# A 2-layer encoder on one core: the mixer's output projection as seven block products in place of eight

## The chip, the cores and the metric

One core of a Trainium2 chip runs one program that computes both layers. The metric is the device time of one execution in microseconds. The kernel before was run three times for its time, and once more with the hardware profiler; the profiled execution has a time of its own.

## The reference, cut to what matters

Each layer does, on x (512 tokens x 1024 channels, float32):

```python
x = x + 0.5 * swiglu(rms_norm(x, ffn1_norm[l]), ffn1_w_in[l], ffn1_w_out[l])
x = x + token_mixer(rms_norm(x, mix_norm[l]), ...)      # ends with the lines below
x = x + 0.5 * swiglu(rms_norm(x, ffn2_norm[l]), ffn2_w_in[l], ffn2_w_out[l])
# token_mixer:
merged = gates[:, :, 0] * y_pool + gates[:, :, 1] * y_attn + gates[:, :, 2] * y_lru
return merged @ w_out                                    # 512x1024 by 1024x1024
```

After two layers there is one more RMS norm. The change is in `merged @ w_out`, once in each layer, and in how its result is added to x.

## The kernel before, in words

Every matrix product keeps float32 accuracy by a split: a float32 operand becomes a high part (ScalarE copies it to the rounded type fp32r) and a low part (VectorE subtracts the high part from the operand), and three matmuls (high by high, high by low, low by high) stand for one. Weights come from HBM into a buffer called `raw` (128x1024, 512 KB) and are split into `wh` and `wl`; the low part of merged and of other activations is made in the same way.

The work is a list of `Unit`s, each with a weight block, its matmuls (`mm`) and what follows them (`after`). The loop at the end of the program issues a unit's matmuls and then calls `gap`, which issues, in this order: what was put off with `later`, the unit's `after` (evictions of its result), the tasks that `defer(n, ...)` set for this gap, the ScalarE half of the split of the unit three ahead (`splits_to(done[-1] + 3)`), the side work of attention and the recurrence, what was put off with `later`, and the VectorE half of that split. Each engine runs its instructions in the order in which they are issued. After a split `loads()` fetches further blocks on SP's queue as far as the limit `held` lets it. All 128x1024 buffers come from one pool of 43 (`BIGS`); all matmul results from 8 PSUM banks.

The feed-forward networks already compute their products by a Strassen-Winograd scheme, in `seven`: the left operand A and the weight W are cut in 2x2 blocks, and seven block products P1, P2, Q5, Q3, P6, P7, Q4 take the place of eight. The left operands are A11, A12, A22 and the sums S1 = A21 - A22, S2 = S1 - A11, S3 = A11 - A21, S4 = A12 + S2. The sums of weight blocks are made by an accumulating DMA of the POOL queue (`add_fn`), which adds a block from HBM onto a `raw` that a product before has just been split from (`acc`): W11 becomes W11+W12 for Q5, then +W22 for P6, then +W21 for Q4, and W22 becomes W22+W12 for P7. The results are added to x block by block (`put`, `total`).

The output projection before is a plain product: for each column half (`ch` 1, then 0) four weight blocks of two 128-row slices, each a unit of 24 matmuls (4 row tiles x 2 slices x 3). In the second half the last two blocks' matmuls are held back, so that the row tiles 2 and 3 end first. `evict` then does x = 0.5 * result + x, one VectorE operation for each of the 8 row tiles, and calls `done(hh, ch)`, which starts the next feed-forward network on that quarter of x: squares for the norm on ScalarE, transposes on TensorE one gap later (`z_block`), and the sums and splits of z (`z_ready`). Merged's blocks are made by `y1(cpair)`, four units just ahead of the projection: gate times branch plus the other branches, then high and low part into `st["mg"]`.

In the profile, tiles are named by the program: `o` is the projection's result, `mg` merged, `y` a branch product, `zt`, `zf`, `zs`, `zh`, `zl` the next network's input (transposed, copied, summed, high, low), `P` and `Q` the block products. All instructions of the helpers have line 83, so the groups are told apart by tile names.

Of the kernel before, what the change touches and what calls it, by code (L numbers as in the profile page):

```python
# [17 lines left out]
S = 512  # L18
# [88 lines left out]
def trunk_kernel(ctx, tc, xn, pm, fin, cst, bd, f1i, f1o, win, wbp, wba, wbl, wout, f2i, f2o, out):  # L107
# [70 lines left out]
    x = {}  # L178
# [230 lines left out]
    LEFT = {"P1": "A11", "P2": "A12", "Q5": "S1", "Q3": "S4", "P6": "S2", "P7": "S3", "Q4": "A22"}  # L409

    def seven(order, nk, width, left, wap, after, held, prep=None, fresh=False):
# [6 lines left out]
        for p in order:  # L418
            name = LEFT[p]
            for n, (k0, k1) in enumerate(parts):  # L420
# [12 lines left out]
                elif p == "Q4":  # L433
                    block = b1[n]
                elif p == "P2":
                    block = Block([ld(1, 0)])
                elif p == "Q3":
                    block = b2[n] = Block([ld(1, 1)])
                    acc = ap(0, 1)
                else:  # L440
                    block = b2[n]
# [19 lines left out]
                units.append(Unit(block, flat((k1 - k0) * width), mm, fin, acc=acc, held=held[p] if isinstance(held, dict) else held, nk=k1 - k0))  # L461


    def ffn(wi, wo, done, order0, rf, lim0=12):
# [131 lines left out]
        comb, U, u, q5 = {}, {}, {}, {}  # L596
# [40 lines left out]
        def prep(p, n, i):  # L637
            if n % 2 == 0:
                sums, parts = combos(LEFT[p], n // 2)
                if LEFT[p] in ("S1", "S4", "S3"):  # L640
                    add_hook(i - 4, sums)
                add_hook(i - 3, parts)
            else:
                add_hook(i, lambda k=(LEFT[p], n // 2): comb.pop(k))

        def put(hh, kk, src, sign=1.0):
            for tt in range(2):
                xv = x[2 * (hh ^ rf) + tt, kk]
                V.scalar_tensor_tensor(out=xv, in0=src[tt], scalar=0.25 * sign, in1=xv, op0=MUL, op1=ADD)

        def copies(dst):
            def fn(ps):
                dst.update(enumerate(two("u")))
                for tt in range(2):
                    A.activation(out=dst[tt], in_=ps[tt], func=AF.Copy)
            return fn

        def total(ps):
            for tt in range(2):
                V.tensor_tensor(out=u[tt], in0=ps[tt], in1=u[tt], op=ADD)  # L660

        def o_p1(ps):
            copies(u)(ps)
            later.append(lambda: put(0, 0, u))

        def o_p2(ps):
            later.append(lambda: put(0, 0, ps))
            defer(1, lambda: done(0 ^ rf, 0))

        def o_q5(ps):  # L670
            copies(q5)(ps)
            later.append(lambda: put(0, 1, q5))
            defer(1, lambda: later.append(lambda: put(1, 1, q5)))
            defer(2, q5.clear)

        def o_q3(ps):
            later.append(lambda: put(0, 1, ps))

        def o_p6(ps):
            later.append(lambda: (total(ps), put(0, 1, u, -1.0)))  # L680
            defer(1, lambda: done(0 ^ rf, 1))

        def o_p7(ps):
            later.append(lambda: (total(ps), put(1, 1, u, -1.0)))
            defer(1, lambda: (later.append(lambda: (put(1, 0, u), u.clear())), done(1 ^ rf, 1)))

        def o_q4(ps):
            put(1, 0, ps)
            done(1 ^ rf, 0)
# [5 lines left out]
        def left(name, k):  # L695
# [3 lines left out]
              {"P1": o_p1, "P2": o_p2, "Q5": o_q5, "Q3": o_q3, "P6": o_p6, "P7": o_p7, "Q4": o_q4},  # L699
# [3 lines left out]
    def mixer(l, side, done, between):  # L703
# [344 lines left out]
        def after_gate(b, c):  # L1048
            def fn(ps):
                if c % 2 == 0:  # L1050
                    g["gt", b] = two("gt")
# [45 lines left out]
        def y1(cpair):  # L1097
# [18 lines left out]
            def after():  # L1116
                if cpair == 0:
                    st["mg"] = [None] * KD
                for s in range(2):
# [458 lines left out]
```

## Time and profile before

| what | before |
|---|---|
| time, median of three runs (lowest to highest) | 2153.4 us (2152.71 to 2156.05) |
| time of the profiled execution, its span | 2148.72 us, 2147.0 us |
| ScalarE and POOL busy | 1192.8 us, 343.4 us |
| bytes moved by DMA, mean rate | 314.61 MB, 147 GB/s |
| granted TensorE clock, mean | 0.995 |

The span runs from the first to the last instruction. "Busy" is the time in which at least one instruction of the engine runs; a matmul's record is longer than its share of the engine, since matmuls overlap, so that the pace is read from start to start. In a row of a timeline the bracket tells how long the engine stood idle before the instruction, and what ended the idle time. In the tables by stretch "x217" counts instructions.

### The profile page before, as it was taken

What the parts mean: (1) busy time and instruction counts of PE and PEld (TensorE: products, weight loads), DVE (VectorE), ACT (ScalarE), POOL (GpSimd) and SP (SyncE); (2) the same over time, 40 slices, a digit from 0 to 9 for tenths busy, and PEclk for the clock granted to TensorE, in tenths of its full rate; (3) what the DMA queues carried; (4) which work ended last, traced back from release to release, by engine and by line L of the source; (5) the groups of instructions that cost most, each with busy time, mean ns of one, the idle gap of its engine ahead of it and who ended that gap; (6) DMA issues with size and microseconds to landing.
All of it is one profiled execution on the core that took longest, in us unless ns stands there. A gap on an engine that the chain in (4) does not pass through costs nothing. (4 is left out here: it accounts for less than half of the span.)

```text
span 2147.0 us, 26106 instructions
## 1 busy us (share of the span) xinstructions
PE 2086.4 (97%) x9648; PEld 1735.6 (81%) x9648; DVE 1658.0 (77%) x2355; ACT 1192.8 (56%) x1763; POOL 343.4 (16%) x292
## 2 busy tenths in 40 slices
PE   7999999999999999999999999999999999999998
PEld 5888888788787878987878988877887877888786
DVE  5877898598677487779977778976967766877797
ACT  6554565646563554546665555565455536555564
POOL 1222230000000022322312222300000000222230
PEclk9999999999999999999999999999999999999999
DMA  8888896122225278898967889941221353888894
GB/s 224 181 153 191 196 200 180 50 79 88 67 81 172 78 141 169 165 200 206 207 162 142 170 179 232 185 127 60 79 79 59 116 154 84 175 151 193 203 177 106
DMA packets 194096, 314.61 MB, mean 147 GB/s; under 512 B 10544, under 2 KB 86832, under 8 KB 193968
## 3 DMA queue, kind: packets, MB, share of 16 engines
q0 software_dynamic: 76288, 138.43, 38.9%
q1 hardware_dynamic: 117680, 174.51, 24.9%
q8 instruction: 75, 1.23, 0.2%
q14 instruction: 53, 0.43, 0.1%
HBM read 310.80 MB, written 2.10 MB: 146 GB/s over the span
## 5 line engine op out<-in xcount | busy, mean ns | idle before, releaser
L83 DVE TENSOR_TENSOR wl<-raw,wh 128x1024 fp32r<-128x1024 f32 (+2 forms) x696 | 709.1, 1038 | 204.6 <-ACT wh L83 202.4
L83 ACT ACTIVATE wh<-raw 128x1024 fp32r<-128x1024 f32 (+2 forms) x696 | 610.5, 906 | 264.5 <-DMA raw<-in_f1i_dram 115.4
L83 PE MATMUL ps<-z,wh 128*128 128x512 f32 x1216 | 380.1, 393 | 0.0
L371 POOL DMA_DIRECT2D raw<-in_f2i_dram x96 | 115.9, 1223 | 1133.5 <-DVE wl L83 390.1
L83 PE MATMUL P<-wl,zh 128*128 128x512 f32 (+1 forms) x768 | 287.5, 374 | 8.3 <-DVE wl L83 8.3
L83 PE MATMUL P<-wh,zh 128*128 128x512 f32 (+1 forms) x768 | 286.9, 374 | 2.1 <-ACT wh L83 2.1
L83 PE MATMUL P<-wh,zl 128*128 128x512 f32 (+1 forms) x768 | 285.9, 372 | 0.0
L83 PEld LDWEIGHTS ps<-z,wh 128*128 128x128 f32 x1216 | 227.1, 188 | 51.0 <-issue 3.4
L83 PE MATMUL ps<-z,wl 128*128 128x512 f32 x608 | 237.0, 390 | 0.0
L83 PE MATMUL Q<-wl,zh 128*128 128x512 f32 (+1 forms) x576 | 218.5, 379 | 14.5 <-DVE wl L83 14.5
L83 PE MATMUL Q<-wh,zh 128*128 128x512 f32 (+1 forms) x576 | 221.0, 384 | 7.5 <-ACT zh L83 3.9
L83 PE MATMUL Q<-wh,zl 128*128 128x512 f32 (+1 forms) x576 | 217.1, 377 | 5.4 <-DVE zl L83 5.4
L371 POOL DMA_DIRECT2D raw<-in_f1i_dram x96 | 116.0, 1232 | 377.8 <-DVE wl L83 276.5
L83 PEld LDWEIGHTS P<-wl,zh 128*128 128x128 f32 x768 | 144.5, 188 | 33.7 <-DVE wl L83 14.0
L83 PEld LDWEIGHTS P<-wh,zh 128*128 128x128 f32 x768 | 144.5, 188 | 24.3 <-ACT wh L83 4.4
L83 PEld LDWEIGHTS P<-wh,zl 128*128 128x128 f32 x768 | 144.6, 188 | 19.6
L83 PE MATMUL P<-wl,ah 128*128 128x512 f32 x352 | 138.2, 393 | 3.3 <-DVE wl L83 3.1
L83 PEld LDWEIGHTS Q<-wl,zh 128*128 128x128 f32 x576 | 109.6, 190 | 37.1 <-DVE wl L83 22.9
L83 PE MATMUL P<-wh,ah 128*128 128x512 f32 x352 | 137.4, 390 | 0.0
L83 PE MATMUL P<-wh,al 128*128 128x512 f32 x352 | 137.2, 390 | 0.0
L83 PEld LDWEIGHTS ps<-z,wl 128*128 128x128 f32 x608 | 114.1, 188 | 23.7
L83 PEld LDWEIGHTS Q<-wh,zh 128*128 128x128 f32 x576 | 109.8, 191 | 25.1 <-ACT zh L83 5.6
(189 smaller groups left out, 3412.2 us busy)
## 6 DMA issues: line engine op xcount, KB each, us to landing
raw<-in_win_dram SPq DMA_DIRECT2D x84, 512.0 KB, 4.3
raw<-in_f1i_dram POOLq DMA_DIRECT2D x64, 512.0 KB, 7.2
raw<-in_f2i_dram POOLq DMA_DIRECT2D x64, 512.0 KB, 6.9
raw<-in_f2i_dram SPq DMA_DIRECT2D x52, 512.0 KB, 5.1
raw<-in_f1i_dram SPq DMA_DIRECT2D x50, 512.0 KB, 5.8
raw<-in_f1o_dram POOLq DMA_DIRECT2D x40, 512.0 KB, 8.0
raw<-in_f2o_dram POOLq DMA_DIRECT2D x40, 512.0 KB, 8.2
raw<-in_f1o_dram SPq DMA_DIRECT2D x30, 512.0 KB, 7.3
```

Of the source, the lines that this page charges most:

```text
L83: return fn(*args, **kw)
L371: return lambda raw: GP.dma_start(out=raw[:, 0:n * w].rearrange("p (k f) -> p k f", f=w), in_=src, accum_op=ADD)
```

## The change

The projection goes through `seven`, with merged as the left operand and `w_out` as the weight, both cut in 2x2 blocks (256 tokens x 512 channels; 512 x 512). A product is two units of 12 matmuls (2 row tiles x 2 slices x 3), in the order P1, P2, Q5, P7, P6, Q3, Q4. S1 to S4 of merged's blocks are made by `m_sum` from the float32 merged, which the gates' tiles keep in `st["mf"]`, in the gaps 1, 2, 4 and 6 behind the last `y1` (S1, S3, S2, S4), each with its own high and low part. Since P7 stands ahead of Q3, its block is loaded as W22 with W12 added at once, and Q3 loads W22 anew. The functions that add the products to x are moved out of `ffn` into `added`, shared by both; with `seventh` they take other orders. The row halves are exchanged (`rf = 1`): quarters of x are ready in the order A22 (behind P2), A11 (one gap behind P6), A21 (Q3), A12 (Q4).

```diff
-    LEFT = {"P1": "A11", "P2": "A12", "Q5": "S1", "Q3": "S4", "P6": "S2", "P7": "S3", "Q4": "A22"}
+    SEVEN = {"P1": "A11", "P2": "A12", "Q5": "S1", "Q3": "S4", "P6": "S2", "P7": "S3", "Q4": "A22"}
 
     def seven(order, nk, width, left, wap, after, held, prep=None, fresh=False):
...
                     block = b2[n] = Block([ld(1, 1)])
-                    acc = ap(0, 1)
+                    acc = ap(0, 1) if order.index("P7") > order.index("Q3") else None
+                elif order.index("P7") < order.index("Q3"):
+                    block = Block([ld(1, 1)], ap(0, 1))
                 else:
                     block = b2[n]

...
+    def added(scale, rf, done, seventh=False):
+
+
+        u, q5 = {}, {}
+
+        def put(hh, kk, src, sign=1.0):
+            for tt in range(2):
+                xv = x[2 * (hh ^ rf) + tt, kk]
+                V.scalar_tensor_tensor(out=xv, in0=src[tt], scalar=scale * sign, in1=xv, op0=MUL, op1=ADD)
+
+        def copies(dst):
+            def fn(ps):
+                dst.update(enumerate(two("u")))
+                for tt in range(2):
+                    A.activation(out=dst[tt], in_=ps[tt], func=AF.Copy)
+            return fn
+
+        def total(ps):
+            for tt in range(2):
+                V.tensor_tensor(out=u[tt], in0=ps[tt], in1=u[tt], op=ADD)
+
+        def p1(ps):
+            copies(u)(ps)
+            later.append(lambda: put(0, 0, u))
+            if seventh:
+                defer(1, lambda: later.append(lambda: put(0, 1, u, -1.0)))
+
+        def p2(ps):
+            later.append(lambda: put(0, 0, ps))
+            defer(1, lambda: done(0 ^ rf, 0))
+
+        def q5_(ps):
+            copies(q5)(ps)
+            later.append(lambda: put(0, 1, q5))
+            defer(1, lambda: later.append(lambda: put(1, 1, q5)))
+            defer(2, q5.clear)
+
+        def q3(ps):
+            if seventh:
+                put(0, 1, ps)
+                return done(0 ^ rf, 1)
+            later.append(lambda: put(0, 1, ps))
+
+        def p6(ps):
+            if seventh:
+                later.append(lambda: (total(ps), put(1, 1, u, -1.0), put(0, 1, ps, -1.0)))
+                return close22()
+            later.append(lambda: (total(ps), put(0, 1, u, -1.0)))
+            defer(1, lambda: done(0 ^ rf, 1))
+
+        def p7(ps):
+            if seventh:
+                return later.append(lambda: total(ps))
+            later.append(lambda: (total(ps), put(1, 1, u, -1.0)))
+            close22()
+
+        def close22():
+            defer(1, lambda: (later.append(lambda: (put(1, 0, u), u.clear())), done(1 ^ rf, 1)))
+
+        def q4(ps):
+            put(1, 0, ps)
+            done(1 ^ rf, 0)
+
+        return {"P1": p1, "P2": p2, "Q5": q5_, "Q3": q3, "P6": p6, "P7": p7, "Q4": q4}
...
                 if c % 2 == 0:
-                    g["gt", b] = two("gt")
+                    gt = big(name="gt")
+                    g["gt", b] = [gt[:, 0:S], gt[:, S:2 * S]]
+                    if b == 1:
+                        st["mf"][c // 2] = gt
...
+                if cpair == 3:
+                    defer(1, lambda: m_sum("S1"))
+                    defer(2, lambda: m_sum("S3"))
+                    defer(4, lambda: m_sum("S2"))
+                    defer(6, lambda: m_sum("S4"))
...
-        for ch in (1, 0):
-            box = {"held": []}
-            for u4 in range(4):
-                b = Block([load_fn(wout[l][u4 * 256:u4 * 256 + 256, ch * S:(ch + 1) * S].rearrange("(k p) f -> p k f", p=128), 2, S)])
-
-                def part(ts, box):
-                    for t in ts:
-                        for k0, uh, ul in box["held"]:
-                            for k in (k0, k0 + 1):
-                                wh, wl = (a[:, (k - k0) * S:(k - k0 + 1) * S] for a in (uh, ul))
-                                th, tl = (a[:, t * 128:(t + 1) * 128] for a in st["mg"][k])
-                                PE.matmul(box["ps"][t], lhsT=th, rhs=wh, start=k == 0, stop=False)
-                                PE.matmul(box["ps"][t], lhsT=th, rhs=wl, start=False, stop=False)
-                                PE.matmul(box["ps"][t], lhsT=tl, rhs=wh, start=False, stop=k == KD - 1)
-
-                def mm(u, a0, a1, u4=u4, ch=ch, box=box):
-                    if u4 == 0:
-                        box["ps"] = [bank("o") for _ in range(4)]
-                    box["held"].append((2 * u4, u.hi, u.lo))
-                    if ch == 0 and u4 >= 2:
-                        if u4 == 3:
-                            part((2, 3), box)
-                        return
-                    part(range(4), box)
-                    box["held"].clear()
-
-                def evict(hh, ch, box):
-                    for tt in range(2):
-                        t = 2 * hh + tt
-                        V.scalar_tensor_tensor(out=x[t, ch], in0=box["ps"][t], scalar=0.5, in1=x[t, ch], op0=MUL, op1=ADD)
-                    done(hh, ch)
-
-                def after(u4=u4, ch=ch, box=box):
-                    if u4 == 3:
-                        evict(1, ch, box)
-                        if ch == 1:
-                            evict(0, ch, box)
-                            box.clear()
-
-                units.append(Unit(b, flat(), mm, after, held=8))
-
-        def last_mm(u, a0, a1, box=box):
-            part((0, 1), box)
-            box["held"].clear()
-            st["mg"] = None
-
-        def last_after(box=box):
-            evict(0, 0, box)
-            box.clear()
-
-        units.append(Unit(None, [], last_mm, last_after))
+        rf = 1
+        sums = {}
+
+        def m_block(name):
+
+            if name in sums:
+                return [sums[name][:, j * S:(j + 1) * S].rearrange("p (c q) -> p c q", c=2) for j in range(2)]
+            r, k = (int(name[1]) - 1) ^ rf, int(name[2]) - 1
+            return [t.rearrange("p (c q) -> p c q", c=2)[:, :, r * 256:r * 256 + 256] for j in range(2) for t in (st["mf"][2 * k + j],)]
+
+        def m_sum(name):
+            a, b, op = {"S1": ("A21", "A22", SUB), "S2": ("S1", "A11", SUB), "S3": ("A11", "A21", SUB), "S4": ("A12", "S2", ADD)}[name]
+            a, b = m_block(a), m_block(b)
+            t = sums[name] = big(name="ms")
+            for o, p, q in zip(m_block(name), a, b):
+                V.tensor_tensor(out=o, in0=p, in1=q, op=op)
+            hi, lo = big(F32R, "mh"), big(F32R, "ml")
+            A.activation(out=hi, in_=t, func=AF.Copy)
+            later.append(lambda: V.tensor_tensor(out=lo, in0=t, in1=f(hi), op=SUB))
+            mc[name] = (hi, lo)
+            if name == "S4":
+                sums.clear()
+                st["mf"].clear()
+
+        mc = {}
+
+        def left(name, k):
+            if name[0] == "S":
+                return [a[:, k * 256:k * 256 + 256] for a in mc[name]]
+            r, c = (int(name[1]) - 1) ^ rf, 4 * (int(name[2]) - 1) + k
+            return [a[:, r * 256:r * 256 + 256] for a in st["mg"][c]]
+
+        def wap(r, c, k0, k1):
+            return wout[l][r * 512 + k0 * 128:r * 512 + k1 * 128, c * S:(c + 1) * S].rearrange("(k p) f -> p k f", p=128)
+
+        results = added(0.5, rf, done, True)
+
+        def then(p):
+            def fn(ps):
+                results[p](ps)
+                mc.pop(SEVEN[p], None)
+                if p == "P1":
+                    st["mg"][0:4] = [None] * 4
+                if p == "Q4":
+                    st["mg"] = None
+            return fn
+
+        seven(["P1", "P2", "Q5", "P7", "P6", "Q3", "Q4"], 4, S, left, wap, {p: then(p) for p in results}, 10)
```

In `ffn` the functions `o_p1` to `o_q4`, `put`, `copies` and `total` go, and `added(0.25, rf, done)` takes their place with the same operations.

## Rows read from the trace of the kernel before

**Rows 1.** Page, busy time by engine: busy us, share of the span, instructions.
```profile
PE 2086.4 (97%) x9648; PEld 1735.6 (81%) x9648; DVE 1658.0 (77%) x2355; ACT 1192.8 (56%) x1763; POOL 343.4 (16%) x292
```

**Rows 2.** Busy time by stretch: us, then each engine's busy us, PEclk, DMA share, GB/s.
```profile
692.20:738.30 46.10, 46.10 (x217) 38.48 (x216) 22.96 (x33) 19.37 (x36) 0.00 (x0) 1.00 0.34 99
738.30:781.00 42.70, 36.57 (x157) 27.49 (x155) 33.30 (x41) 25.11 (x36) 7.22 (x6) 1.00 0.65 144
1749.50:1795.60 46.10, 46.10 (x214) 38.35 (x213) 23.13 (x33) 19.08 (x35) 0.00 (x0) 1.00 0.35 100
1795.60:1838.00 42.40, 37.34 (x162) 28.18 (x160) 33.51 (x41) 26.13 (x38) 7.23 (x6) 1.00 0.66 148
```

**Rows 3.** Timeline of TensorE, layer 0: start, us, operation, count.
```profile
692.23 0.39 PE L83 MATMUL o<-wh,mg 128*128 128x512 f32 x1
...
719.43 1.91 PE L83 MATMUL zt<-cst,x 128*128 128x128 f32 x16
...
721.09 0.48 PE L83 MATMUL o<-wh,mg 128*128 128x512 f32 x1
...
738.31 0.47 PE L83 MATMUL P<-wh,zh 128*128 128x512 f32 x1
```

**Rows 4.** Timeline of VectorE, projection of layer 0: [idle before, releaser].
```profile
699.30 4.63 DVE L83 TENSOR_TENSOR wl<-raw,wh 128x1024 fp32r<-128x1024 f32 x4 [0.26 <-ACT wh L83]
...
712.82 0.69 DVE L83 SCALAR_TENSOR_TENSOR x<-o,x 128x512 f32<-128x512 f32 x1 [8.89 <-PE o L83]
...
733.75 0.16 DVE L83 TENSOR_TENSOR m<-m 128x2 f32<-128x2 f32 x1 [0.79 <-ACT q L83]
...
735.34 1.23 DVE L83 TENSOR_TENSOR wl<-raw,wh 128x1024 fp32r<-128x1024 f32 x1
```

**Rows 5.** Timeline of VectorE, first feed-forward block of layer 0.
```profile
743.38 1.22 DVE L83 TENSOR_TENSOR zs<-zf 128x1024 f32<-128x1024 f32 x1
...
745.72 1.22 DVE L83 TENSOR_TENSOR zl<-zs,zh 128x1024 fp32r<-128x1024 f32 x1 [1.12 <-ACT zh L83]
...
764.78 1.28 DVE L83 TENSOR_TENSOR c<-P,u 128x512 f32<-128x512 f32 x2
```

**Rows 6.** Groups by line and form: busy us, mean ns; idle before.
```profile
L83 ACT ACTIVATE wh<-raw 128x1024 fp32r<-128x1024 f32 x404 | 416.6, 1052 | 173.8 <-DMA raw<-in_f1i_dram 72.7 <-DMA raw<-in_f2i_dram 58.6 <-DVE wl L83 26.8
...
L83 ACT ACTIVATE u<-P 128x512 f32<-128x512 f32 x40 | 23.6, 604 | 29.5 <-PE P L83 29.2
```

**Rows 7.** Timeline of ScalarE, layer 0.
```profile
698.22 3.89 ACT L83 ACTIVATE wh<-raw 128x1024 fp32r<-128x1024 f32 x4
...
773.20 1.06 ACT L83 ACTIVATE wh<-raw 128x1024 fp32r<-128x1024 f32 x1 [3.12 <-DMA raw<-in_f2i_dram]
```

**Rows 8.** Timeline of TensorE, first feed-forward block of layer 0.
```profile
745.74 0.50 PE L83 MATMUL Q<-wh,zh 128*128 128x512 f32 x1 [0.81 <-ACT zh L83]
...
747.00 0.50 PE L83 MATMUL Q<-wh,zl 128*128 128x512 f32 x1 [0.52 <-DVE zl L83]
...
757.44 0.50 PE L83 MATMUL P<-wl,zh 128*128 128x512 f32 x1 [0.95 <-DVE wl L83]
```

**Rows 9.** DMA queues and issues (count, KB each, median us from issue to landing).
```profile
q0 software_dynamic: 76288, 138.43, 38.9%
q1 hardware_dynamic: 117680, 174.51, 24.9%
...
raw<-in_f2i_dram POOLq DMA_DIRECT2D x64, 512.0 KB, 6.9
...
raw<-in_f2o_dram POOLq DMA_DIRECT2D x40, 512.0 KB, 8.2
...
raw<-in_f2o_dram POOLq DMA_DIRECT2D x8, 256.0 KB, 10.4
```

More of the change, by code (lines that the diff above doesn't have):

```diff
@@ L418, in seven @@
         for p in order:
-            name = LEFT[p]
+            name = SEVEN[p]
             for n, (k0, k1) in enumerate(parts):
@@ L593, in ffn @@
         add_hook(nz, zc.clear)
-        comb, U, u, q5 = {}, {}, {}, {}
+        comb, U = {}, {}
         cols = [1024, 1024, 768]
@@ L638, in prep @@
             if n % 2 == 0:
-                sums, parts = combos(LEFT[p], n // 2)
-                if LEFT[p] in ("S1", "S4", "S3"):
+                sums, parts = combos(SEVEN[p], n // 2)
+                if SEVEN[p] in ("S1", "S4", "S3"):
                     add_hook(i - 4, sums)
@@ L643, in prep @@
             else:
-                add_hook(i, lambda k=(LEFT[p], n // 2): comb.pop(k))
-        def put(hh, kk, src, sign=1.0):
-            for tt in range(2):
[L648 to L689, printed above, removed]
+                add_hook(i, lambda k=(SEVEN[p], n // 2): comb.pop(k))
+        results = added(0.25, rf, done)
         def wap(r, c, k0, k1):
@@ L698, in ffn @@
         seven(later_order, KF // 2, S, left, wap,
-              {"P1": o_p1, "P2": o_p2, "Q5": o_q5, "Q3": o_q3, "P6": o_p6, "P7": o_p7, "Q4": o_q4},
+              results,
               dict(P1=12, P2=14, Q5=14, Q3=14, P6=14, P7=12, Q4=9), prep)
@@ L1180, in mixer @@
         units[n0].between = between
-        for ch in (1, 0):
-            box = {"held": []}
-            for u4 in range(4):
-                b = Block([load_fn(wout[l][u4 * 256:u4 * 256 + 256, ch * S:(ch + 1) * S].rearrange("(k p) f -> p k f", p=128), 2, S)])
-                def part(ts, box):
-                    for t in ts:
-                        for k0, uh, ul in box["held"]:
-                            for k in (k0, k0 + 1):
-                                wh, wl = (a[:, (k - k0) * S:(k - k0 + 1) * S] for a in (uh, ul))
-                                th, tl = (a[:, t * 128:(t + 1) * 128] for a in st["mg"][k])
-                                PE.matmul(box["ps"][t], lhsT=th, rhs=wh, start=k == 0, stop=False)
-                                PE.matmul(box["ps"][t], lhsT=th, rhs=wl, start=False, stop=False)
-                                PE.matmul(box["ps"][t], lhsT=tl, rhs=wh, start=False, stop=k == KD - 1)
-                def mm(u, a0, a1, u4=u4, ch=ch, box=box):
-                    if u4 == 0:
-                        box["ps"] = [bank("o") for _ in range(4)]
-                    box["held"].append((2 * u4, u.hi, u.lo))
-                    if ch == 0 and u4 >= 2:
-                        if u4 == 3:
-                            part((2, 3), box)
-                        return
-                    part(range(4), box)
-                    box["held"].clear()
-                def evict(hh, ch, box):
-                    for tt in range(2):
-                        t = 2 * hh + tt
-                        V.scalar_tensor_tensor(out=x[t, ch], in0=box["ps"][t], scalar=0.5, in1=x[t, ch], op0=MUL, op1=ADD)
-                    done(hh, ch)
-                def after(u4=u4, ch=ch, box=box):
-                    if u4 == 3:
-                        evict(1, ch, box)
-                        if ch == 1:
-                            evict(0, ch, box)
-                            box.clear()
-                units.append(Unit(b, flat(), mm, after, held=8))
@@ L1386, in between @@
             flush()
+        st["mf"] = {}
         mixer(l, side, to_ffn(g2, 0), between)
```

## The prediction

> **What bounds the kernel now.** I read the page's engine summary first: TensorE is busy for 97% of the span and VectorE for 77% [rows 1], which says that removed matmuls should pay, but it is a mean over stages. So I went to the busy time by stretch [rows 2], with the stretch edges taken from the first output-projection matmul of each layer and the first matmul of the feed-forward network behind it (692.2 and 738.3 us in layer 0; 1749.5 and 1795.6 in layer 1). In the projection TensorE is busy 46.1 of 46.1 us while VectorE is busy 23 of 46, so there TensorE alone sets the pace. In the first 43 us behind it TensorE has 6.1 us of gaps and VectorE is at 33.3 of 42.7: that seam is set by VectorE and the handovers between it and ScalarE. Third, the timelines of the engines. TensorE goes straight from 692.23 to 738.31 at 0.227 us a matmul (120 from 692.23 to the transposes at 719.43) [rows 3]. VectorE comes late into the stage: the last branch tiles' evictions hold it until 699.3, 7 us after TensorE began on the projection; then it does four weight splits in a row (4.63 us) and finds nothing more to do until 712.8 [rows 4]. So before the change the projection starts with VectorE about three units of work behind, and survives that because units here are 24 matmuls long (5.44 us) and a unit's split is made three units ahead.
>
> **The change, part by part.** All numbers are for one layer, for one profiled execution (2148.7 us around a span of 2147.0); it ran 4.7 us under the median of the three timed runs, so I carry the difference over to 2153.4.
>
> *Matmuls.* Before, 2 column halves x 8 k-blocks x 4 row tiles x 3 = 192. After, 7 products x 4 k-blocks x 2 row tiles x 3 = 168. 24 x 0.227 = 5.44 us of TensorE go. The transposes ahead of the feed-forward network are 24 before and after, 0.83 us for eight (16 from 719.43 to 721.09 [rows 3]).
>
> *VectorE.* A full-width operation (128x1024) takes 1.22 us and a half-width one (128x512) 0.69; what they cost in the queue is less, since they overlap: four in 4.63 us are 1.14 each [rows 4], two half-width ones in 1.28 are 0.60 each [rows 5]. Splits: 14 units in place of 8, so 6 x 1.14 = 6.8 us more. Adding results to x: P1 4, P2 2, Q5 4, P7 2, P6 6 and 2 one unit later, Q3 2, Q4 2 = 24 half-width operations in place of 8: 16 x 0.60 = 9.6 us more. Sums S1 to S4 of merged's blocks: two half-width sums and one full-width low part each, 4 x (1.20 + 1.14) = 9.4 us. Together 25.8 us more VectorE work in a stage that gets 5.4 us shorter for TensorE. ScalarE gets six splits and four high parts more at 1.05 us, four in 3.89, so 0.95 each in the queue, and four copies at 0.60 [rows 6, 7]: about 11.7 us.
>
> *Cover.* The new work could hide in VectorE's idle time: 46.1 - 23.0 = 23 us in the projection and 42.7 - 33.3 = 9.4 us behind it [rows 2]. The second part is mostly not free: it is the wait between a sum, its high part on ScalarE and its low part on VectorE (1.12 us behind the sum at 743.38, and three times more) [rows 5]. So 25.8 us stand against 23 us of cover, and the cover is not where the work is: a unit is now 12 matmuls, 2.72 us, and "split three units ahead" is 8.2 us in place of 16.3.
>
> *The walk.* I number the new units 1 to 14 (P1, P2, Q5, P7, P6, Q3, Q4, two each) and write down each engine's queue in the order in which the code issues it, with the durations above. Behind unit n stand its evictions, the sum that is due there (S1 behind unit 1, S3 behind 2, S2 behind 4, S4 behind 6), and the split of unit n+3. VectorE's queue behind units 1 to 12 is 3.5, 4.7, 2.3, 4.7, 1.1, 4.7, 2.3, 2.3, 1.1, 4.7, 2.3, 3.4 = 37.3 us (1.1 of the last are the small ops of the row norms, as from 733.75 to 735.34, less the wait in them [rows 4]). TensorE begins unit 1 at 692.23. Unit 3's low part is the first of the four splits, done at 700.5, and TensorE wants it at 697.7: it waits for the high part until 699.3 and for the low part again, 2.7 us in all. From here each step repeats: the sum, its high part, then the split's high part on ScalarE, then two low parts on VectorE. Waits: unit 4 2.0 (split done at 705.2), unit 5 2.0 (709.9), unit 7 0.8 (717.0; the transposes of A22 cover the rest), unit 9 2.8 (725.2: two copies, S4's high part and four transposed tiles stand ahead of its split on ScalarE), the first feed-forward matmul 1.4 (A11's high part stands behind the rsqrt and the four copies). Sum 11.6 us. 692.2 + 14 x 2.72 + 3 x 0.83 + 11.6 = 744.4, against 738.3 before: the 5.4 us saved are gone and 6.2 more. The same walk with the queues of before gives 738.3 for that matmul and 746.6 for the first of Q5; the trace has 738.31 and 745.74 [rows 3, 8], so I trust it to about 1 us at this seam.
>
> *Behind the seam.* Nothing gives it back. The feed-forward network's block sums wait on VectorE before too (0.81 and 0.52 us, and 0.95 for a split [rows 8]); with VectorE arriving late they only shift. S1 of z now comes one unit earlier relative to the first feed-forward matmul, but in the same queue entry as Q4's eviction and a split. The walk carried on gives the first matmul of Q5 7.4 us late and the last product of the first block 6.2 to 6.5 us late; I take 6.2. Behind that TensorE is the bound and a delay stays.
>
> *Transfers.* Weights: SP still loads eight times 512 KB (W22 twice, W12 no longer by SP), the POOL queue adds eight accumulating transfers of 512 KB. Neither wait nor cost of these is in the trace for these weights. By nearest rows an accumulating transfer lands 6.9 to 8.2 us after issue, 10.4 in the slowest group [rows 9]. The tight ones are P6's and Q4's: each is issued when the split before is done (709.9, 725.2) and read four units later (ScalarE at 722.8 and 733.5). At 6.9 and at 8.2 us the walk gives the same; at 10 it gives 1.8 us more at the seam and 3.6 more by the end of the first block, at 12 3.8 and 7.6. I take 8.2, the feed-forward output weights' row, since these transfers come equally dense. ScalarE's idle time on such a transfer, 3.12 us at 773.20 [rows 7], shows that this distance of four units is just at the edge before, too. The P7 pair and the first Q5 pair are issued early enough. SP's loads for the feed-forward network come later than before, since W11's two buffers stay held until Q4, but 3 or more units ahead; I cost that at 0, and if it fails it adds to the 12 us case.
>
> Sum: 2 layers x 6.2 = 12.4 us: 2161.1 in the profiled execution's terms, 2165.8, so 2166, against the median. Layer 1 has the same busy times at the same places [rows 2], so the factor of two holds.
>
> **Rivals.**
> 1. *TensorE stays the bound.* VectorE keeps up, each layer gains 5.44 us: 2153.4 - 10.9 = 2142.5. For it: 97%, and 23 us of idle VectorE. Against: it needs all of the 25.8 us to be done inside the stage without any wait, and VectorE's queue begins 8 us behind. It decides if the split of unit 3 is done by 697.7. Half of it, 2148, if VectorE catches up behind the seam. The Trainium skill (Perfetto Trace Analysis, section Identifying the Most-Contended Engine) judges TensorE by its weight-load share, other engines by occupancy, and says to optimise the fullest one first; in the projection's stretch that is 38.5 of 46.1 us, 83%, against VectorE's 50% [rows 2], and by that rule this rival would be the forecast. The rule looks at the stage as it was; the queue of the changed stage is another.
> 2. *VectorE binds, but without its bubbles.* Its queue from 700.4 us plus 37.3 us and A11's low part (1.14) ends at 738.9, where the first feed-forward matmul stood before: nothing gained or lost, 2153, at most 4 to either side. For it: puts and copies can fill the time in which a high part is awaited. Against: the walk already lets them.
> 3. *Transfers land late.* At 12 us a transfer each layer loses 6.2 + 7.6: 2153.4 + 27.6 = 2181; at 10 2173. For it: an accumulating transfer takes more of the DMA engines than a plain one (38.9% of the time for 138 MB against 24.9% for 175 MB [rows 9]), and POOL's queue is in order, with the feed-forward network's own accumulations, which wait for their loads, standing ahead of P6's. Against: the DMA share in the stage is 0.34 [rows 2].
>
> **How the numbers follow.** The main case 0.53 (its own range 2160 to 2172), transfers 0.17, no change 0.15, TensorE bound or half of it 0.15. The main case and the transfers are slower by over 0.2% (4.3 us, about what can be told from no change here); so slower 0.70, same 0.16, faster 0.14. The range 2150 to 2177 leaves out the full gain and the late end of the transfers.
>
> **What would show it.** Right: gaps on TensorE in the projection, 8 to 12 us a layer where there were none, nearly all ended by a VectorE or ScalarE split, the first before P2; VectorE without long idle stretches there; first feed-forward matmul about 52 us after the first projection matmul instead of 46.1; 168 matmuls. Wrong: TensorE closed through the projection, or gaps ended by a transfer (rival 3), or gaps there that are won back by fewer waits in the first feed-forward block.

## The result, and the profile after

The changed kernel takes 2172.0 us (median of four runs, 2171.8 to 2173.6) against 2153.1 for the kernel before (four runs, 2150.9 to 2156.1): a ratio of 1.0089 (95% interval 1.0071 to 1.0106), 19.0 us slower. The forecast was 2166, 12.6 slower. The profiled execution took 2173.64 us around a span of 2171.9.

The page of the changed kernel, busy time by engine and DMA queues, which answer to [rows 1] and [rows 9]:

```profile
PE 2087.5 (96%) x9600; PEld 1730.5 (80%) x9600; DVE 1709.8 (79%) x2423; ACT 1215.7 (56%) x1791; POOL 362.8 (17%) x308
...
q0 software_dynamic: 80640, 146.82, 40.8%
q1 hardware_dynamic: 117680, 174.51, 24.8%
```

48 matmuls fewer, 68 VectorE instructions more, 8.4 MB more by accumulating transfers. Busy time by stretch of the changed kernel, layer 0 and then layer 1. The edges are the first projection matmul, the first feed-forward matmul and the end of the first feed-forward block, which is its first transposes of `ht`:

```profile
691.90:744.50 52.60, 45.12 (x193) 34.69 (x191) 45.10 (x63) 29.40 (x48) 8.49 (x7) 0.97 0.72 167
744.50:792.00 47.50, 39.75 (x166) 29.78 (x166) 38.64 (x47) 29.23 (x41) 7.22 (x6) 1.00 0.60 130
1763.60:1815.30 51.70, 43.60 (x194) 33.55 (x192) 44.95 (x63) 29.43 (x48) 8.49 (x7) 1.00 0.74 171
1815.30:1863.10 47.80, 39.55 (x165) 29.73 (x166) 38.90 (x48) 29.08 (x41) 7.22 (x6) 1.00 0.59 129
```

In the kernel before, the edges of [rows 2] are not all at these events: the blocks end at 783.56 and 1841.06, and in layer 1 the first matmuls of the projection and of the feed-forward network come at 1750.30 and 1796.38, 0.8 us later than the prediction has them. At the events the kernel before reads as follows (block of layer 0, projection and block of layer 1):

```profile
738.30:783.60 45.30, 39.17 (x168) 29.58 (x167) 34.84 (x43) 27.61 (x38) 7.22 (x6) 1.00 0.64 144
1750.30:1796.40 46.10, 46.10 (x218) 38.50 (x216) 22.94 (x33) 19.32 (x36) 0.00 (x0) 1.00 0.34 99
1796.40:1841.10 44.70, 39.21 (x168) 29.55 (x166) 35.91 (x45) 27.61 (x38) 7.23 (x6) 1.00 0.64 145
```

The projection is 6.5 us longer in layer 0 and 5.6 in layer 1. TensorE, busy throughout before, now has 7.5 to 8 us of gaps there, and VectorE went from 23 us busy to 45. The block behind also became longer: 47.4 and 47.8 us where before it is 45.3 and 44.7, though its code is the same. Timeline of TensorE, changed kernel, layer 0 (start, us, operation; in brackets the idle time and what ended it), which answers to [rows 3]:

```profile
698.96 0.49 PE L83 MATMUL P<-wh,mg 128*128 128x512 f32 x1 [1.42 <-ACT wh L83]
700.22 0.50 PE L83 MATMUL P<-wl,mg 128*128 128x512 f32 x1 [0.77 <-DVE wl L83]
703.52 0.50 PE L83 MATMUL P<-wh,mg 128*128 128x512 f32 x1 [0.52 <-ACT wh L83]
704.97 0.51 PE L83 MATMUL P<-wl,mg 128*128 128x512 f32 x1 [0.95 <-DVE wl L83]
708.21 0.49 PE L83 MATMUL Q<-wh,mh 128*128 128x512 f32 x1 [0.41 <-ACT wh L83]
709.66 0.50 PE L83 MATMUL Q<-wl,mh 128*128 128x512 f32 x1 [0.95 <-DVE wl L83]
...
716.75 0.50 PE L83 MATMUL P<-wl,mh 128*128 128x512 f32 x1 [0.47 <-DVE wl L83]
...
723.49 0.50 PE L83 MATMUL P<-wh,mh 128*128 128x512 f32 x1 [1.25 <-ACT wh L83]
724.75 0.50 PE L83 MATMUL P<-wl,mh 128*128 128x512 f32 x1 [0.76 <-DVE wl L83]
...
726.39 0.63 PE L83 MATMUL P<-wl,mh 128*128 128x512 f32 x1
...
744.52 0.50 PE L83 MATMUL P<-wh,zh 128*128 128x512 f32 x1
...
789.30 0.50 PE L83 MATMUL Q<-wl,zh 128*128 128x512 f32 x1 [2.24 <-DVE wl L83]
```

Nine waits, every one ended by a weight split, first its high part on ScalarE, then its low part on VectorE (before unit 7 the low part alone): before the units 3, 4, 5, 7 and 9, where the walk put them. From start to start, less the pace of 0.227, the units lose 2.6, 1.9, 1.8, 0.7 and 2.4 us: 9.5 in all. The row at 726.39 is of another kind: its matmul lasts 0.63 and the next begins 0.43 us later. Windows of 1 us there (last but two: granted clock):

```profile
725.00:726.00 1.00, 1.00 (x5) 0.80 (x5) 1.00 (x3) 1.00 (x2) 0.66 (x1) 1.00 0.05 17
726.00:727.00 1.00, 1.00 (x4) 0.81 (x3) 1.00 (x2) 0.28 (x1) 0.54 (x1) 0.51 0.00 0
727.00:728.00 1.00, 1.00 (x4) 0.81 (x3) 1.00 (x3) 0.00 (x0) 0.66 (x1) 0.50 0.85 55
```

TensorE's granted clock fell from 2.4 to 1.2 GHz behind the two waits of unit 9 and came back at 729.4. With a mean of 0.97 over the 52.6 us that costs 1.7 us. In layer 1 the same nine waits stand there with the same lengths and the clock stays at 1.00; a wait of 0.8 us ahead of the first feed-forward matmul comes in instead. The two together make the difference between 52.6 and 51.7.

Why the splits are late shows on VectorE and ScalarE, changed kernel, layer 0 [rows 4, 7]:

```profile
698.94 1.23 DVE L83 TENSOR_TENSOR wl<-raw,wh 128x1024 fp32r<-128x1024 f32 x1 [0.26 <-ACT wh L83]
700.08 1.29 DVE L83 TENSOR_TENSOR ms<-gt 128x512 f32<-128x512 f32 x2
702.55 1.23 DVE L83 TENSOR_TENSOR ml<-ms,mh 128x1024 fp32r<-128x1024 f32 x1 [1.19 <-ACT mh L83]
703.70 1.22 DVE L83 TENSOR_TENSOR wl<-raw,wh 128x1024 fp32r<-128x1024 f32 x1
```

```profile
701.46 1.06 ACT L83 ACTIVATE mh<-ms 128x1024 fp32r<-128x1024 f32 x1 [2.56 <-DVE ms L83]
702.43 1.04 ACT L83 ACTIVATE wh<-raw 128x1024 fp32r<-128x1024 f32 x1
...
731.58 1.06 ACT L83 ACTIVATE wh<-raw 128x1024 fp32r<-128x1024 f32 x1 [5.30 <-DMA raw<-in_wout_dram]
...
781.56 1.06 ACT L83 ACTIVATE wh<-raw 128x1024 fp32r<-128x1024 f32 x1 [4.35 <-DMA raw<-in_f2i_dram]
```

Read the first two ScalarE rows with the VectorE rows: ScalarE idles 2.56 us for the sum S1, then makes its high part, and only then the split of unit 4 that stands behind it. VectorE in turn idles 1.19 us for that high part, with a split's low part behind. ScalarE waits so for each of the four sums (2.56, 1.72, 4.14 and 1.59 us); VectorE waits for the high part of the first alone, as its queue is full behind that. The 5.30 us at 731.58 is a wait for a transfer in the projection; no TensorE wait follows it. The one at 781.56 is in the feed-forward block.

### The profile page after: what moved, and what is told of

It reads as the page before. It is cut to its first block, busy times and chain, and to the rows that moved or that the text cites. A ratio compares the mean times of both kernels' runs of the same rounds, so it can differ in the third digit from the quotient of the medians.

```text
span 2171.9 us, 26169 instructions
## 1 busy us (share of the span) xinstructions
PE 2087.5 (96%) x9600; PEld 1730.5 (80%) x9600; DVE 1709.8 (79%) x2423; ACT 1215.7 (56%) x1791; POOL 362.8 (17%) x308
## 3 DMA queue, kind: packets, MB, share of 16 engines
q8 instruction: 75, 1.23, 0.2%
## 5 line engine op out<-in xcount | busy, mean ns | idle before, releaser
L83 DVE TENSOR_TENSOR wl<-raw,wh 128x1024 fp32r<-128x1024 f32 (+2 forms) x708 | 724.7, 1043 | 203.9 <-ACT wh L83 202.7
L83 ACT ACTIVATE wh<-raw 128x1024 fp32r<-128x1024 f32 (+2 forms) x708 | 622.6, 909 | 288.3 <-DMA raw<-in_f1i_dram 120.8
L83 PE MATMUL Q<-wl,zh 128*128 128x512 f32 (+1 forms) x576 | 220.1, 382 | 22.1 <-DVE wl L83 22.1
L83 PEld LDWEIGHTS P<-wh,zl 128*128 128x128 f32 x768 | 144.6, 188 | 21.5 <-DVE zl L83 1.9
L371 POOL DMA_DIRECT2D raw<-in_wout_dram x16 | 19.2, 1203 | 773.9 <-DVE gt L83 674.3
L83 PEld LDWEIGHTS Q<-wl,zh 128*128 128x128 f32 x576 | 110.2, 191 | 44.5 <-DVE wl L83 30.4
```

The source lines that it names most:

```text
L83: return fn(*args, **kw)
L371: return lambda raw: GP.dma_start(out=raw[:, 0:n * w].rearrange("p (k f) -> p k f", f=w), in_=src, accum_op=ADD)
```

## The experiments

The table has the two stretches of each kernel, read as above, layer 0 / layer 1, and how much of them went to the half clock (1 less the granted clock, times the length). It is what the verdicts rest on, beside the times. e1 to e12 are the experiments below, in this order.

| kernel | projection, us | first block behind, us | of these, half clock, us |
|---|---|---|---|
| before | 46.1 / 46.1 | 45.3 / 44.7 | 0 / 0 |
| changed | 52.6 / 51.7 | 47.4 / 47.8 | 1.7 / 0 |
| e1 | 52.5 / 52.6 | 48.4 / 47.1 | 6.6 / 1.7 |
| e2 | 45.3 / 43.7 | 49.6 / 48.7 | 5.1 / 3.4 |
| e3 | 43.6 / 43.6 | 48.2 / 46.6 | 3.3 / 0 |
| e4 | 47.3 / 47.3 | 47.3 / 47.8 | 1.7 / 1.7 |
| e5 | 55.9 / 55.3 | 48.3 / 47.6 | 9.7 / 6.8 |
| e6 | 54.0 / 54.1 | 47.7 / 47.2 | 6.8 / 6.8 |
| e7 | 48.8 / 45.8 | 49.1 / 48.1 | 5.1 / 1.3 |
| e8 | 52.6 / 51.7 | 44.5 / 44.4 | 3.4 / 0 |
| e9 | 46.1 / 46.1 | 43.9 / 43.9 | 0 / 0 |
| e10 | 45.4 / 44.6 | 48.8 / 47.1 | 5.0 / 1.7 |
| e11 | 46.2 / 48.5 | 47.6 / 48.5 | 3.4 / 4.8 |
| e12 | 46.0 / 45.7 | 44.1 / 44.4 | 3.4 / 3.4 |

All ratios are against the kernel before in the same series of runs; its median lies between 2150.2 and 2153.1 in these series, so that times of two series can be compared to some 3 us only.

**The accumulating transfers of the projection.** `seven` for the projection without the added blocks:

```diff
-                ap = lambda r, c, k0=k0, k1=k1: add_fn(wap(r, c, k0, k1), k1 - k0, width)
+                ap = lambda r, c, k0=k0, k1=k1: add_fn(wap(r, c, k0, k1), k1 - k0, width) if add else None
...
```

> The changed kernel without the eight accumulating transfers of a layer's projection: the seven products read W11, W21, W22 as loaded, so the weights of Q5, P7, P6 and Q4 are wrong. Theory (VectorE's queue and its handovers to ScalarE hold TensorE): the waits of TensorE in the projection stay where they are, 9 to 11 us a layer, the first feed-forward matmul comes 52 us behind the first projection matmul; time 2168 to 2173, at most 2 us a layer less, from less DMA traffic behind. Rival (the accumulating transfers hold the splits): the waits go, 8 to 10 us a layer, time 2152 to 2158.

2172.1 us, ratio 1.0105 [1.0084, 1.0126]: no faster than the changed kernel. The waits for splits stay (1.39 and 0.76 before unit 3, 1.25 and 0.76 before unit 9). These transfers are not the cause, and rival 3 falls for the projection.

**The sums of merged's blocks.** Left operands are plain blocks, `m_sum` is never called:

```diff
-                if cpair == 3:
-                    defer(1, lambda: m_sum("S1"))
...
+            name = {"S1": "A22", "S2": "A12", "S3": "A12", "S4": "A22"}.get(name, name)
```

> The changed kernel without the sums S1 to S4 of merged's blocks: plain blocks stand in their place (Q5, P6, Q4 with A22, P7 with A12), so the result is not the reference's. Same matmuls, splits, additions to x and transfers; VectorE has 9.4 us less a layer and four handovers sum, high part, low part are gone. Theory (VectorE's queue): the wait ahead of P2 (2.2 us) stays, as the queue is late from the stage before; those ahead of P2's second unit, Q5, P7 and P6 go, 6 to 7 us a layer; time 2157 to 2161. Rival (transfers): no change, 2172. Rival (the order in which the quarters of x come makes the seam worse): the projection gets 6 us shorter but the first feed-forward block loses as much again, 2168 to 2172.

2155.7 us, 1.0027 [1.0014, 1.0040]. The projection falls from 52.6 and 51.7 to 45.3 and 43.7; of its waits only the first pair is left (1.43 and 0.76). So the sums make all the others. e2 takes the work of the sums away together with their hand-overs, so it does not tell the two apart. Yet both blocks behind lost two stretches of half clock, 3.4 us each, and that took much of what was won.

**Sums and the added results.** As e2, and with `seventh` four of the `put`s (eight half-width additions to x a layer) left out:

```diff
-            if seventh:
-                defer(1, lambda: later.append(lambda: put(0, 1, u, -1.0)))
...
-                later.append(lambda: (total(ps), put(1, 1, u, -1.0), put(0, 1, ps, -1.0)))
+                later.append(lambda: (total(ps), put(1, 1, u, -1.0)))
```

> The same and, besides, 8 of the 24 additions to x left out (P1's and Q5's second, P6's second, the one behind P6), so 14.2 us less VectorE work a layer than in the changed kernel; TensorE's work unchanged. Theory (VectorE's queue): TensorE waits only ahead of P2 in the projection, and the 5.4 us a layer of removed matmuls begin to show: 2146 to 2153, at or below the kernel before (2153). Rival (transfers): 2168 to 2172. Rival (order of the quarters of x): stays above 2160.

2152.0 us, 1.0009 [0.9992, 1.0027]: level with the kernel before. The projection is 2.5 us shorter than before in both layers, which is TensorE's own saving of 5.4 us less, for the most part, the first pair of waits. It is won and given back in the block: in layer 0 2.9 us, with 3.3 us of half clock in it, in layer 1 1.9 us at the full clock.

**Earlier splits.** The last eight units before the projection look further ahead, so that the projection's first splits are made in the mixer:

```diff
+        for n, u in zip([5, 6, 7, 7, 7, 6, 5, 4], units[-len([5, 6, 7, 7, 7, 6, 5, 4]):]):
+            u.look = n
...
-            for fn in splits_to(done[-1] + 3):
+            for fn in splits_to(done[-1] + units[done[-1]].look):
```

> The changed kernel with the splits of the projection's first four units made ahead of the last branch products' evictions, in VectorE's idle time at 660 to 680 us; the result is the reference's. Theory (VectorE's queue begins the stage late): the waits ahead of P2 (2.2 and 1.5 us) go or shrink, and 2 to 4.5 us a layer are won: 2163 to 2168. Rival (transfers): no change, 2172, or slower if the earlier splits bring the first accumulating transfers into the loads. Rival (only the handovers count, not where the queue begins): the waits move to Q5 and nothing is won.

2162.5 us, 1.0065 [1.0044, 1.0086], with all the arithmetic of the changed kernel. It is 9.6 us under e1 in the same series; by the ratios it is 5 us under the changed kernel, and their intervals overlap. The waits before units 3 and 4 are gone, that before unit 9 stays, and one before unit 10 comes in (1.17 and 0.76; 0.33 and 0.76). The mixer's stage ahead became 2.5 us longer a layer (327.4 against 325.0); one stretch of half clock, 1.7 us, is in it.

**The sums on GpSimd.** As e4, with the sums and their low parts on GpSimd:

```diff
-                V.tensor_tensor(out=o, in0=p, in1=q, op=op)
+                GP.tensor_tensor(out=o, in0=p, in1=q, op=op)
...
-            later.append(lambda: V.tensor_tensor(out=lo, in0=t, in1=f(hi), op=SUB))
+            GP.tensor_tensor(out=lo, in0=t, in1=f(hi), op=SUB)
```

> The kernel of e4 (first four splits early) with the sums S1 to S4 and their low parts on GpSimd in place of VectorE; the result is the reference's. It is e2 with nothing left out: VectorE has 9.4 us less a layer, the handover sum, high part, low part stays but no longer in VectorE's queue. Theory (VectorE's queue): no wait ahead of P2 and hardly one in the projection, the first feed-forward matmul 41 to 44 us behind the first projection matmul (52 in the changed kernel, 46.1 before), 3 to 5 us a layer off e4: 2152 to 2157. Rival (GpSimd is too slow, or slows VectorE where both read the buffers): S1 comes after TensorE needs it for Q5, waits ended by GpSimd, 2162 or more.

2181.7 us, 1.0143 [1.0129, 1.0158]: a miss, the slowest of all, and both parts of the rival show. The tile `ms` in its trace (engine, operation, count: shortest, median and longest in ns, first and last start), and who waited for it (us, times):

```profile
L1231 POOL TENSOR_TENSOR ms<-gt x8: 1597/1704/1740, 693.4 to 1780.0; 128x512 f32<-128x512 f32 x8
...
L1234 POOL TENSOR_TENSOR ml<-ms,mh x8: 2356/2378/2400, 701.1 to 1803.3; 128x1024 fp32r<-128x1024 f32 x8
L1231 POOL TENSOR_TENSOR ms<-ms,gt x4: 3149/3160/3167, 714.9 to 1791.0; 128x512 f32<-128x512 f32 x4
L1231 POOL TENSOR_TENSOR ms<-gt,ms x4: 2249/2254/2256, 722.8 to 1799.9; 128x512 f32<-128x512 f32 x4
...
  ACT mh L83: 35.7, 8
```

Each high part stands on ScalarE ahead of a weight split and now waits for a slower sum: 35.7 us in eight waits, where e4 has 18.4. And VectorE was not relieved: it has 11 operations fewer in the projection of layer 0 than in e4 (46 against 57) and is busy for 38.85 us against 39.14, since its splits and additions last longer where a GpSimd operation runs beside them. The stretch in e4 and in e5, and one such pair in e5:

```profile
692.40:739.70 47.30, 42.66 (x194) 33.57 (x192) 39.14 (x57) 26.13 (x44) 7.33 (x6) 1.00 0.80 215
696.10:752.00 55.90, 47.38 (x193) 37.27 (x191) 38.85 (x46) 26.09 (x44) 28.91 (x17) 0.88 0.71 182
...
708.05 2.36 POOL L1234 TENSOR_TENSOR ml<-ms,mh 128x1024 fp32r<-128x1024 f32 x1 [1.17 <-ACT mh L83]
708.95 2.54 DVE L83 TENSOR_TENSOR wl<-raw,wh 128x1024 fp32r<-128x1024 f32 x1 [3.22 <-ACT wh L83]
```

That split takes 1.21 to 1.23 us where GpSimd is idle. Of each layer's projection 6.8 us are half clock besides. What each of the three costs was not separated.

**GpSimd and later squares.** As e5, and the squares for the norm three units later (`defer(wait, ...)`):

> e5 with the squares for the next norm put off by three units (ScalarE's eight squares and the small VectorE operations no longer stand ahead of the last splits of the projection). Theory of the seam (the second part of the loss, 2 to 4 us a layer in the first feed-forward block, is ScalarE's and VectorE's queue at the last four units, where four quarters of x now come close together): 1.5 to 3 us a layer less than e5, 2147 to 2153, at or below the kernel before. Rival (the loss in the block comes from its own accumulating transfers, which start when the splits of Q3 and P6 come in a bunch): no change against e5.

2179.2 us, 1.0134 [1.0121, 1.0147]: a miss, little changed against e5. This is what its rival has, that the loss in the block comes from the block's own transfers.

**Earlier splits and later squares.** e4 with the squares three units later:

```diff
-            squares(hh, kk)
+            if wait:
+                defer(wait, lambda: squares(hh, kk))
+            else:
+                squares(hh, kk)
```

> e4 with the same put-off of the squares, sums on VectorE as in the changed kernel. Theory of the seam: 1.5 to 3 us a layer less than e4's 2162.5, so 2157 to 2160. Rival (transfers of the block): 2162.

2160.7 us, 1.0057 [1.0042, 1.0071]; the interval overlaps that of e4, so nothing is shown for the squares.

**The block's own accumulations.** In the changed kernel, and in the kernel before, the first block of each layer's second feed-forward network without the accumulating transfers for P6, P7 and Q4:

```diff
+                acc = acc if add else None
...
-        ffn(f2i[l], f2o[l], to_out if last else to_ffn(lambda m, l=l: pc(l + 1, "g1", m), 1), ["P1", "Q5", "P2", "Q3", "P6", "P7", "Q4"], 0)
+        ffn(f2i[l], f2o[l], to_out if last else to_ffn(lambda m, l=l: pc(l + 1, "g1", m), 1), ["P1", "Q5", "P2", "Q3", "P6", "P7", "Q4"], 0, second=True)
```

> The changed kernel, and in the first block of the second feed-forward network the accumulating transfers for P6, P7 and Q4 left out (their weights are then wrong). From the first feed-forward matmul to the first transposes of its output the changed kernel takes 47.4 and 47.8 us in the two layers, the kernel before 45.3 and 44.7. Theory (the second part of the loss comes from these transfers: they are issued later and closer together, and the split of P7's second half waits for one): 44 to 45 us, 2 to 3 us a layer less, time 2165 to 2168. Rival (VectorE's queue with the sums of z): 47 us still, 2171.

> The same left out in the kernel before. Theory of the transfers: it waits for them less, so it wins only about 1 to 2 us a layer (its last wait of 1.4 us): stretch 43.5 to 44.5 us, time 1 to 4 us under the kernel before; after that the two kernels' stretches are alike within 0.7 us. Rival: both lose the same, and the difference of 2 to 3 us between them stays.

e8 2161.9 us, 1.0050 [1.0031, 1.0069]; e9 2146.4 us, 0.9986 [0.9972, 0.9999]. Without these transfers the block takes 44.5 and 44.4 us in the changed kernel and 43.9 in the one before: within 0.6 of each other (1.7 of the 44.5 are half clock), where with them they stand 2.2 and 3.1 apart. By the ratios the two kernels lie 0.64% apart without these transfers and 0.89% with them, some 5 us of the 19. So the transfers make the difference, and the traces show how. POOL's issues for P7's and Q4's halves, the changed kernel and then the one before:

```profile
769.93 1.20 POOL L371 DMA_DIRECT2D raw<-in_f2i_dram  x1 [11.05 <-DVE wl L83]
772.44 1.20 POOL L371 DMA_DIRECT2D raw<-in_f2i_dram  x1 [1.30 <-PE Q L83]
774.53 1.21 POOL L371 DMA_DIRECT2D raw<-in_f2i_dram  x1 [0.89 <-DVE wl L83]
777.72 1.20 POOL L371 DMA_DIRECT2D raw<-in_f2i_dram  x1 [1.99 <-DVE wl L83]
```

```profile
760.54 1.20 POOL L371 DMA_DIRECT2D raw<-in_f2i_dram  x1 [9.69 <-DVE wl L83]
765.17 1.20 POOL L371 DMA_DIRECT2D raw<-in_f2i_dram  x1 [3.42 <-DVE wl L83]
768.63 1.20 POOL L371 DMA_DIRECT2D raw<-in_f2i_dram  x1 [2.26 <-DVE wl L83]
770.97 1.20 POOL L371 DMA_DIRECT2D raw<-in_f2i_dram  x1 [1.14 <-DVE wl L83]
```

A late VectorE makes the block's splits late and bunched, and each accumulation waits for the split of the buffer it adds to: the four go out in 7.8 us in place of 10.4. They land 6.2, 9.0, 10.8 and 11.4 us after issue, before 8.3, 8.0, 8.5 and 9.6. P7's second half is read 9.1 us after issue (772.44 to 781.56) in place of 8.0, and the last wait of the block on TensorE is 2.24 us (789.30) where before it is 1.37:

```profile
780.93 0.50 PE L83 MATMUL Q<-wl,zh 128*128 128x512 f32 x1 [1.37 <-DVE wl L83]
```

The way from that reading to the end of the last wait is the same in both kernels, 7.7 us: P7's low part, six operations on the block's results and Q4's low part follow each other on VectorE. So the block's loss stands at the reading. From the block's first matmul it comes 37.0 us behind in place of 34.9 in layer 0, and 37.4 in place of 34.3 in layer 1 (1852.70 and 1830.70): 2.2 and 3.1 us later, all that the block lost. 1.1 us of it in each layer is the later issue, the rest the longer landing. That closer issues make the landing longer fits these rows and was not tested apart.

**High and low part apart from the sum.** e4, with the parts of each sum one unit behind the sum:

```diff
-            hi, lo = big(F32R, "mh"), big(F32R, "ml")
...
+            defer(1, parts)
```

> The kernel of e4 with the high and low part of each sum S1 to S4 issued one unit behind the sum, so that no split of a weight stands on ScalarE behind a high part that waits for VectorE; the result is the reference's, the work is the same. Theory with the handover as a part of it: the 1.2 us that VectorE and ScalarE wait at each sum go and the queue's load is spread evenly; the waits in the projection fall from 6 us a layer to 2 to 3, 2 to 4 us a layer less than e4 (2162.5): 2155 to 2159. Rival (only the amount of VectorE's work counts): 2161 to 2163.

2161.5 us, 1.0046 [1.0032, 1.0060]. The projection falls as expected, to 45.4 and 44.6, under that of the kernel before; the total hardly moves, a miss. The block stays at 48.8 and 47.1, with the transfers in it, and 6.7 us of half clock stand in the stretches of the two layers.

**The same and later squares.**

> e10 with the squares for the norm put off by three units as in e7. Theory: 1 to 2 us less than e10 as e7 was under e4: 2153 to 2158, so at best equal to the kernel before (2151 to 2153). Rival (what is left is in the transfers of the first feed-forward block): equal to e10.

2162.9 us, 1.0048 [1.0031, 1.0065]: no gain.

**P7's block without an accumulation onto a split buffer.** e10, and in the first blocks of the second network of each layer and of layer 1's first (`fresh`) P7 gets its own buffer, W22 with W12 added at load:

```diff
-                elif order.index("P7") < order.index("Q3"):
+                elif order.index("P7") < order.index("Q3") or fresh:
                     block = Block([ld(1, 1)], ap(0, 1))
```

> e10 with, in each feed-forward network's first block that starts with P1, Q5, the weight of P7 loaded as W22 with W12 added at once (a block of its own), in place of the accumulation that waits for Q3's split; the result is the reference's. Theory (the second part of the loss is the wait for the accumulating transfers behind Q3's and P6's splits): from the first feed-forward matmul to the first transposes 45 to 47 us in place of 47 to 49, 1 to 2.5 us a layer less than e10: 2156 to 2160; not below the kernel before (2152), as the early splits cost the stage ahead 2.5 us. Rival (the block's transfers are bound by their bandwidth, not by when they are issued): two more loads a block make it equal to or slower than e10, 2161 to 2165.

2150.8 us (12 runs), ratio 0.9999 [0.9982, 1.0016]: 19 us under the changed kernel by the ratios, level with the one before, and better than expected. In the block the waits for the last splits are gone, and Q4's two transfers, now alone, land 7.5 and 6.9 us after issue. It is the best version with seven products; none was faster than the kernel before. The share of layer 1's first network in this was not separated. Its stretches, projection and block of each layer:

```profile
695.00:741.10 46.10, 43.39 (x195) 35.05 (x194) 39.42 (x57) 26.41 (x45) 9.76 (x8) 0.96 0.91 223
741.10:785.20 44.10, 40.17 (x166) 30.76 (x165) 39.19 (x48) 28.63 (x40) 4.81 (x4) 0.96 0.58 137
1747.20:1793.00 45.80, 43.53 (x194) 34.77 (x192) 40.30 (x59) 26.13 (x44) 9.79 (x8) 0.96 0.91 225
1793.00:1837.40 44.40, 40.39 (x166) 30.94 (x166) 39.48 (x49) 28.97 (x41) 4.81 (x4) 0.96 0.58 136
```

The clock is 0.96 in all four, where the kernel before has 1.00: 1.7 us each, 6.8 of TensorE time. If all of that is on the path, the two stretches would without it be 4.0 to 4.6 us a layer under those of the kernel before (an estimate); the stage ahead is 2.7 and 1.2 us longer. That it would then be faster as a whole was not run.

## Why the prediction was right in direction and short in size

*What bounds the projection.* Right. TensorE's weight loads went from 83% of the stretch to 66% (34.69 of 52.60), VectorE from 50% to 86%. Rival 1 falls, and with it the reading of the fullest engine in the stage as it was. Rival 2 falls too: it let VectorE's queue end at 738.9, and the first feed-forward matmul came at 744.52. That the hand-overs have a price of their own shows in e10: with the same work, and the parts of each sum one unit behind it, the projection is 1.9 and 2.8 us shorter than in e4.

*Work added.* VectorE got 25.8 us by the prediction. With the block taken to its end in both kernels, the windows of layer 0 give 22.1 more in the projection and 3.8 in the block, 25.9; those of layer 1 give 22.0 and 3.0.

*The walk.* Right in places and releasers. Forecast 2.7, 2.0, 2.0, 0.8, 2.8 and 1.4 us; measured 2.6, 1.9, 1.8, 0.7, 2.4 and none in layer 0 (0.8 in layer 1). The sum of 11.6 (its terms as rounded add to 11.7) was too high: 9.5 and 10.3. That the first feed-forward matmul came at 744.52 against 744.4 is luck: it owes 1.7 us to the half clock, a term that the sum didn't have; in layer 1, without it, the stretch is 51.7 against the 52.2 of the walk.

*Behind the seam.* This is the step that failed: "Nothing gives it back ... I take 6.2". The delay grew there. At the end of the block it is 8.7 us in each layer (52.6 + 47.4 against 46.1 + 45.3; 51.7 + 47.8 against 46.1 + 44.7), 2.5 more than forecast. e8 and e9 show the cause: the block's own accumulating transfers, which the walk took as landing after 8.2 us whatever their spacing, while I looked for late ones among the projection's. P7's second half was issued 1.1 us later in the block and landed after 9.0 and 9.4 us.

*Transfers.* Costing the projection's at nothing was right (e1); they landed 6.3 us after issue in the median, not 8.2. Rival 3 named the right resource at the wrong place, and its 10 us case had the total, 2173, by another way.

*The sum.* 2 x 8.7 = 17.4 of the 19.0 us. The other 1.6 isn't located. The two profiled executions lie 24.9 apart; of the 7.5 outside these stretches, 3.4 are two more stretches of half clock (four against two, in code that didn't change), and 4.1 stay open. Most of the 7.5 comes in at three places, each beside a fall of the clock that the kernel before doesn't have there (1169.8, 1323.4 and 1893.4 us of the changed kernel's execution).

## What to carry to other kernels

An operation that feeds another engine and waits for it costs its place in both in-order queues, and what stands behind it there pays: walk the queues unit by unit, and put the producer, the hand-over and the consumer in different units before cutting work. Follow a delay into the next stage up to the transfers that its operations trigger, since late releases bunch them. Where an engine was closed before, a change that opens gaps can cost more than the gaps: read the granted clock of the stretch before concluding that a gain got lost in waits.

## What the runs showed of the hardware

TensorE's clock fell in many stretches with gaps, never in the closed projection of the kernel before and of e9. Each fall cost 1.7 us in most cases (matmuls 0.43 us apart in place of 0.227). The profiled kernel before lost 11.3 us to it over the span, the changed one 16.4, e10 21.5. The same nine waits lowered it in layer 0 and not in layer 1, so that no condition is shown. The Trainium skill (TensorE: Matmul & The Clock Gate, section Part 1: The HAM clock gate) says that the clock follows how busy the array has lately been, and that the same kernel meets different numbers of slow matmuls from run to run; the four runs of the changed kernel, with mean granted clocks of 0.989 to 0.992, agree with the second.

GpSimd took 1.70 us in the median for the sums S1 and S3 of 128x512 that VectorE does in 0.68, 2.5 times (S4's records have 2.25, S2's 3.16), and 2.38 against 1.23 for 128x1024, 1.9 times. The Trainium skill (GPSIMD Engine Reference, section 3.1 Elementwise — side-by-side cycle accounting) has 1.96 times for a longer add; the wider form agrees, the half-width one is dearer.

Beside a GpSimd operation VectorE's own took longer. In e5, six of the eight splits that overlap one lasted 2.29 to 2.54 us in place of 1.21 to 1.23, and six half-width additions of `u` to x 1.76 to 2.51 in place of 0.68; e6 has the same lengths.

Four accumulating transfers of 512 KB landed 6.0 to 6.2, 9.0 to 9.4, 10.8 to 11.0 and 11.4 us after issue where they went out within 7.8 us (changed kernel), and after 7.4 to 9.6 where it was 10.4 (kernel before).
